# Layer B, head pairs 1 to 7: the first head's probabilities are split and turned by DMA transposes, the second head's by TensorE

## The chip, the cores and the metric

The kernel runs on one core of one Trainium2 chip. The core has TensorE (matmuls; the trace shows its matmuls as PE and its weight loads as PEld), VectorE (DVE), ScalarE (ACT), GpSimd (POOL) and SyncE (SP), which here does nothing but issue DMAs on one hardware queue, q1. The metric is the device time of one execution in microseconds (us).

## The reference, cut to what matters

The program is one step of a two-layer encoder over 2048 prompt tokens and 64 sample tokens, model width 1024. Each layer is a norm, one projection to q, k, v and a gate, an attention, and an output projection. Layer B has 16 heads of 64, and each chunk of 64 queries sees its own chunk and the 8 before it:

```
# layer B, per head and chunk of 64 queries: band = 8 * 64 + 64 keys
s = q @ k.T * dh ** -0.5 + bias[h, clip(rel, -128, 128)]
p = softmax(s)                 # over the band; keys before the start are masked
o = p @ v
y = x + (o * silu(gate)) @ w_out
```

So each query tile of 128 needs at most five key blocks of 128 (the first four tiles need 1, 2, 3 and 4), and 16 tiles have 70 blocks of 128x128 per head. To multiply by v, TensorE needs p with the keys on the partitions: p has to be transposed, block by block.

## The kernel before, in words

**Layout.** Layer A runs first, then layer B. In layer B the heads go in pairs 0 to 7 (called hp in the code). Within a pair the prompt is cut into units of two query tiles (256 queries), u = 0 to 7, and one unit of sample tokens, NU; the order is u0 to u6, NU, u7. A unit has four steps: tile 0 and tile 1 of head 0, then tile 0 and tile 1 of head 1.

**A step.** `scores` (L1375) multiplies the query tile, kept as two float16 parts, by up to 640 keys into a PSUM tile "sb" (two buffers). DVE adds the bias and takes the negated maximum into p and nm (L1412); ACT takes the exponential and the row sums (L1416). After the last step of a unit DVE takes the reciprocal of the sums (L1422), and POOL multiplies it into the gate, G (L1430). `values` transposes p on TensorE by matmuls against an identity (L840, "sb<-ident,p") into the other "sb" buffer. A product in float16 needs p as two parts: ACT copies the high part, scaled, to ph (L815), and DVE forms the low part in pl (L816). `products` multiplies both parts by v (held in "values") into one PSUM tile "o" (L1503): per head eight matmuls of 256 columns and four of 128 where all blocks are there. After the second head TensorE transposes the gate ("tp<-ident,G"), and ACT, DVE and POOL finish the output (L1243, L1245, L1246), which goes out to a buffer in memory by a DMA, ogb<-o (L1248).

**What sets the order.** TensorE's order is written by hand. A generator, the `filler`, hands out the matmuls of the projections of the next pair (L678 to L680) by a planned cost, and `pipeline` puts the steps of the attention between them: scores of step n, a piece of filler, the transposes of step n-1, with the short products (those of 128 columns and the first) of the head whose p was turned one step earlier laid between them, then that head's other products, then more filler. The other engines' instructions are ordered by a scheduler. SP issues its DMAs in that order, each with its own waits, one after another: the loads of projection inputs (xx<-xsb, 512 KB), weight loads (scan, wl), stores, and the query copies.

**Query copies.** After the second step of a unit, `queries` normalizes and turns the queries of the next unit. One half of the partitions must move to the other half, which is done by two DMAs q<-q of 32 KB (L1352). The first scores of the next unit read what the first of them writes.

Of the kernel before, what the change touches and what calls it, by code (L numbers as in the profile page):

```python
# [11 lines left out]
F16 = mybir.dt.float16  # L12
# [5 lines left out]
P = 128  # L18
# [30 lines left out]
QY = 1  # L49
NS = 4  # L50
HB, WB_, PB, VB = 2.0 ** 10, 2.0 ** 14, 2.0 ** 14, 16.0
LAG = 3
HALF = 5 * 2 * P

@with_exitstack
def hybrid_encoder_kernel(
# [162 lines left out]
    def input_across(h):  # L219
        across(h, h + 1)  # L220
        e, r, o = row[:, 16:17], row[:, 17:18], row[:, 20:23]
        powers(row[:, h : h + 1], e, r)
        times(o[:, 0:1], r, WB_)
        times(o[:, 1:2], e, 1 / (HB * WB_))
        times(o[:, 2:3], e, 0.5 / (VB * PB))

    def input_scales(h):
        everywhere(h, row[:, 20:23])
# [581 lines left out]
    def split_to(dst_hi, dst_lo, src, scale=None):  # L810
# [7 lines left out]
            )  # L818
        return a, b

    def load_cache(ktsrc, vsrc, C, both):
# [12 lines left out]
        nt = C // P  # L834
        for c in range(nt):
            split_to(VS[:, c, :, 0:HD], VS[:, c, :, HD:P], rvv[:, c])
# [415 lines left out]
    def layer_b():  # L1252
# [4 lines left out]
        def add_unit(hp, unit):  # L1257
# [21 lines left out]
            def gen():  # L1279
                xc = st.x.pop((hp, u))  # L1280
                it.prs, it.todo = [], []
                it.gate = t("pb", [P, 2, P], 5)
                if "VH" not in held:
                    held["VH"] = t("values", [P, NT, 2, P], 1, F16)
# [90 lines left out]
        def scores(it, i, h):  # L1375
# [35 lines left out]
            for r, b, c in soft:  # L1411
                mi = nc.vector.tensor_tensor_reduce(  # L1412
                    out=p[r, :nk], in0=S[r, o : o + nk], in1=b,
                    op0=ALU.add, op1=ALU.min, scale=1.0, scalar=3e38, accum_out=it.nm[r, c : c + 1],
                )
            ex = nc.scalar.activation(  # L1416
                p[:n, :nk], p[:n, :nk], AF.Exp,
                scale=-1.0, bias=it.nm[:n, c : c + 1], accum_out=it.sm[:n, c : c + 1],
            )
            bg.anchor(mi, ex)  # L1420
            if c == w - 1:
                nc.vector.reciprocal(it.sm[:n, :w], it.sm[:n, :w])  # L1422
                it.G = G = t("G", [P, 256])
                if u == NU:
                    nc.gpsimd.tensor_tensor(
# [3 lines left out]
                for e in range(len(tiles)):  # L1429
# [3 lines left out]
                        it.sm[:n, 2 * e : 2 * e + 2].unsqueeze(2).to_broadcast([n, 2, HD]),  # L1433
                        op=ALU.mult,
                    )

        def values(it, i, h, short):
            u, T, tiles = it.unit
# [21 lines left out]
            ))  # L1460

        def then(it, i, h):
            if it.unit[0] == NU:
                return [([], lambda: sample_outputs(it)), ([], lambda: sample_turned(it))]
            if i == len(it.unit[2]) - 1:
                return [products(it, h)]
            return []

        def sample_outputs(it):
            O = psum("o", 512, 1)  # L1470
# [11 lines left out]
        def sample_turned(it):  # L1482
# [5 lines left out]
            store(og[1][:, it.hp, SEQ:TOK], o)  # L1488
            finished[1, NU] = finished.get((1, NU), 0) + 1

        def products(it, h):
            u, T, tiles = it.unit
            ta, tb = tiles[0][0], tiles[1][0]
# [16 lines left out]

            def rest():
                if h == 1:
                    n = tiles[0][2]
                    GT = psum("tp", 512, 1)
                    for e, (_, t0, _) in enumerate(tiles):
                        transpose(GT[:, t0 : t0 + n], it.G[:n, e * P : (e + 1) * P])
                    gt = gate_t(GT[:, :T].rearrange("p (j s) -> p j s", j=1), T, G_B(it.hp))
                for y, x in enumerate(full):
                    if y:
                        product(x, 0)  # L1520
                    product(x, 1, stop=y == last)
                if h == 1:
                    finish_pairs(
                        it.O[:, : 2 * T].rearrange("p (j e s) -> p j e s", j=1, e=2),
                        gt,
                        T,
                        og[1][:, it.hp : it.hp + 1, u * UT : u * UT + T],
                        True,
                    )
                    finished[1, u] = finished.get((1, u), 0) + 1  # L1530

            between = [begin]
            for x in short:
# [8 lines left out]
        def pipeline():  # L1542
# [7 lines left out]
            flush()  # L1550
            filler.to(its[1].mark)
            filler.attending = True
            prev, todo = None, []
# [36 lines left out]
            values(*prev, [])  # L1590
            todo += then(*prev)
            while todo:
                filler.to(filler.done + 2.6)
                short, nxt = todo.pop(0)
                for fn in short:
                    fn()
                nxt()
            flush()

        return pipeline  # L1600
# [226 lines left out]
```

## Time and profile before

| | |
|---|---|
| runs of the kernel | 2232.93, 2240.86 and 2242.28 us, median 2240.86 |
| the profiled execution | 2242.53 us, its span 2240.8 us |
| busy in the span: TensorE, weight loads | 96%, 71% |
| busy: DVE, ACT, POOL | 70%, 63%, 38% |
| q1 | 338.10 MB, 49.1% of 16 DMA engines |

All of it is one profiled execution. The rows of the groups give line, engine, operation, output and inputs, the count, then busy us, mean ns of one and idle time before. TensorE's matmuls are pipelined: the spans of neighbours overlap, and the time that one takes away from the others is the distance between two starts. A row of the timeline starts with start and length in us. The stretch from 1200 to 1800 us lies in pairs 2 to 6 of layer B, where the same pattern repeats.

### The profile page before, as it was taken

What the parts mean: (1) busy time and instruction counts of PE and PEld (TensorE: products, weight loads), DVE (VectorE), ACT (ScalarE), POOL (GpSimd) and SP (SyncE); (2) the same over time, 40 slices, a digit from 0 to 9 for tenths busy, and PEclk for the clock granted to TensorE, in tenths of its full rate; (3) what the DMA queues carried; (4) which work ended last, traced back from release to release, by engine and by line L of the source; (5) the groups of instructions that cost most, each with busy time, mean ns of one, the idle gap of its engine ahead of it and who ended that gap; (6) DMA issues with size and microseconds to landing.
All of it is one profiled execution on the core that took longest, in us unless ns stands there. A gap on an engine that the chain in (4) does not pass through costs nothing.

```text
span 2240.8 us, 41683 instructions
## 1 busy us (share of the span) xinstructions
PE 2162.1 (96%) x13931; PEld 1580.2 (71%) x13931; DVE 1567.7 (70%) x4049; ACT 1419.6 (63%) x3610; POOL 858.4 (38%) x1397
## 2 busy tenths in 40 slices
PE   7999999999999999989999999999999999998999
PEld 6877888788889996556666666666566665566888
DVE  6768777667676456878776776867767777677542
ACT  6878778667785333666676666766666667566430
POOL 5545544334354456753333333332332323331000
PEclk9999999999999999999999999999999999999999
DMA  8856547756546666554243342533433424223664
GB/s 269 272 159 215 177 124 220 227 158 187 173 131 190 208 206 232 179 166 128 87 147 110 106 144 76 157 95 97 138 104 113 133 77 126 73 66 99 190 200 126
DMA packets 254072, 340.77 MB, mean 152 GB/s; under 512 B 45648, under 2 KB 191328, under 8 KB 253824
## 3 DMA queue, kind: packets, MB, share of 16 engines
q1 hardware_dynamic: 253856, 338.10, 49.1%
q8 instruction: 110, 1.80, 0.3%
q14 instruction: 106, 0.87, 0.1%
HBM read 257.59 MB, written 73.43 MB: 148 GB/s over the span
## 4 chain that ended last, share of the span: by engine, by line
PE 64%; DVE 13%; ACT 9%; DMA 6%; issue 5%; POOL 3%; SPq 1%; ACTq 0%; DVEq 0%; POOLq 0%
PE pj L678 11%; PE pj L680 11%; PE pj L679 11%; PE pj L1670 4%; PE pj L1672 4%; PE pj L1671 4%; PE sb L840 3%; PE o L1503 3%; PE tp L840 2%; DVE p L1412 2%; DMA scan<-in_w_in_b_dram 2%; PE sa L840 2%; ACT p L1416 2%; DVE pl L816 2%; PE sb L1408 1%
## 5 line engine op out<-in xcount | busy, mean ns | idle before, releaser
L678 PE MATMUL pj<-wh,xx 128*128 128x512 f16 (+2 forms) x1648 | 643.8, 391 | 6.2 <-ACT pb L701 4.8
L680 PE MATMUL pj<-wh,xx 128*128 128x512 f16 (+2 forms) x1648 | 626.1, 380 | 2.5 <-POOL xx L563 2.5
L679 PE MATMUL pj<-wh,xx 128*128 128x512 f16 x1024 | 390.5, 381 | 0.0
L1416 ACT ACTIVATE p<-p,nm 128x640 f32<-128x640 f32 (+5 forms) x264 | 199.5, 756 | 240.1 <-DVE nm L1412 237.5
L1670 PE MATMUL pj<-xx,wh 128*128 128x264 f32 (+1 forms) x1024 | 289.9, 283 | 5.2 <-DVE res L1676 2.2
L1671 PE MATMUL pj<-xx,wh 128*128 128x264 f32 (+1 forms) x1024 | 287.6, 281 | 0.0
L816 DVE SCALAR_TENSOR_TENSOR pl<-sb,ph 128x640 f16<-128x640 f32 (+4 forms) x256 | 189.0, 739 | 97.7 <-ACT ph L815 94.6
L679 PE MATMUL pj<-wl,xx 128*128 128x512 f32 (+1 forms) x624 | 235.7, 378 | 2.5 <-DVE wl L469 2.5
L563 POOL TENSOR_TENSOR xx<-xraw,xx 128x528 fp32r<-128x528 f32 (+4 forms) x144 | 183.9, 1296 | 87.8 <-ACT xx L562 72.8
L840 PE MATMUL sb<-ident,p 128*128 128x128 f32 x1144 | 207.6, 278 | 9.0 <-DVE pl L816 5.7
L1246 POOL TENSOR_TENSOR o<-gt,o 128x256 f32<-128x256 f32 (+1 forms) x132 | 99.9, 757 | 284.1 <-ACT p L1152 91.8
L1412 DVE CUSTOM_DVE_ANT_0 p<-sb,BT 128x640 f32<-128x640 f32 (+5 forms) x272 | 196.1, 721 | 15.5 <-PE sb L1409 10.4
L755 POOL TENSOR_TENSOR sq<-pa 128x256 f32<-128x256 f32 (+2 forms) x187 | 113.1, 605 | 226.0 <-ACT pa L714 152.5
L840 PEld LDWEIGHTS sb<-ident,p 128*128 128x128 f32 x1144 | 149.7, 142 | 68.5 <-DVE pl L816 20.7
L760 POOL TENSOR_TENSOR f<-f,mhalf 128x4 f32<-128x4 f32 (+2 forms) x187 | 192.3, 1028 | 14.1
L815 ACT ACTIVATE ph<-sb 128x640 f16<-128x640 f32 (+4 forms) x256 | 160.3, 626 | 49.8 <-PE sb L840 48.6
L680 PEld LDWEIGHTS <-xx 128*128 128x128 f16 x1024 | 100.7, 98 | 125.3 <-POOL xx L563 3.0
L1152 ACT ACTIVATE p<-p,nm 128x257 f32<-128x257 f32 (+2 forms) x272 | 134.3, 497 | 51.6 <-DVE nm L1146 44.3
L678 PEld LDWEIGHTS <-xx 128*128 128x128 f16 x1024 | 101.0, 99 | 71.4 <-issue 2.5
L679 PEld LDWEIGHTS <-xx 128*128 128x128 f16 x1024 | 100.7, 98 | 70.5 <-issue 2.3
L1503 PE MATMUL o<-pl,values 128*128 128x256 f16 (+1 forms) x672 | 149.5, 255 | 0.0
L1503 PEld LDWEIGHTS <-values 128*128 128x128 f16 x1344 | 134.8, 101 | 15.8 <-issue 0.2
(264 smaller groups left out, 5196.6 us busy)
## 6 DMA issues: line engine op xcount, KB each, us to landing
xx<-xsb SPq DMA_DIRECT2D x112, 512.0 KB, 3.8
xx<-xsa SPq DMA_DIRECT2D x88, 512.0 KB, 4.9
xraw<-oga SPq DMA_DIRECT2D x64, 264.0 KB, 3.8
xraw<-ogb SPq DMA_DIRECT2D x64, 264.0 KB, 3.8
xsa<-xx SPq DMA_DIRECT2D x32, 512.0 KB, 4.1
scan<-in_w_in_b_dram SPq DMA_DIRECT2D x64, 256.0 KB, 4.4
wl<-in_w_in_b_dram SPq DMA_DIRECT2D x64, 256.0 KB, 4.0
xraw<-in_x_dram SPq DMA_DIRECT2D x40, 256.0 KB, 3.9
```

What stands on the lines that cost most here:

```text
L563: nc.gpsimd.tensor_tensor(lo, rv, wide(hi), op=ALU.subtract)
L678: nc.tensor.matmul(ps[:n, :C], xh, wh, start=k == 0, stop=False)
L679: nc.tensor.matmul(ps[:n, :C], xh, wl, start=False, stop=False)
L680: nc.tensor.matmul(ps[:n, :C], xl, wh, start=False, stop=k == KC - 1)
L760: nc.gpsimd.tensor_tensor(fv, fv, mhalf[:n, :H], op=ALU.pow)
L816: b = nc.vector.scalar_tensor_tensor(dst_lo, src, scale, wide(dst_hi), op0=ALU.mult, op1=ALU.subtract)
L840: nc.tensor.transpose(out, in_, ident[:n, :n])
L1412: mi = nc.vector.tensor_tensor_reduce(out=p[r, :nk], in0=S[r, o : o + nk], in1=b, op0=ALU.add, op1=ALU.min, scale=1.0, scalar=3e38, accum_ ...
L1416: ex = nc.scalar.activation(p[:n, :nk], p[:n, :nk], AF.Exp, scale=-1.0, bias=it.nm[:n, c : c + 1], accum_out=it.sm[:n, c : c + 1],)
L1503: nc.tensor.matmul(it.O[:, h * T + q0 : h * T + q1_], vt, p[:, c, q0:q1_], start=start, stop=stop)
L1670: nc.tensor.matmul(ps[:, :OT], wh, oh, start=k == 0, stop=False)
L1671: nc.tensor.matmul(ps[:, :OT], wh, ol, start=False, stop=False)
```

## The change: half of the transposes go to the DMA queue

For pairs 1 to 7 and prompt units, head 0 (`TURNED = (0,)`) takes another way:

- DVE adds log PB to the negated maximum, by one more small operation per step, so that the exponential comes out scaled by PB. The row sums are then scaled too, so one more small DVE operation per unit multiplies their reciprocals by PB.
- `parts` splits p before it is turned: ACT casts the high part to float16, POOL subtracts to get the low part. Both lie in one of three slots that share the tile "values" with v.
- One step later, `turn_p` has SP issue one DMA transpose: up to ten 128x128 blocks (five of each part, 320 KB) go from the slot into the tile "pt" (two buffers). There are 112 such DMAs: seven pairs, eight units, two tiles.
- `turned_products` multiplies by v four steps after the scores of the head's second tile (`LAG = 4`).

Head 1 keeps its transposes on TensorE, but its products come one step later than before, so they are no longer laid between transposes. In these pairs the gate is transposed into an "sb" buffer instead of "tp". The list `todo` with `pop(0)` is replaced by entries with a step number, run by `due`. TensorE has 490 transposes fewer (7 x 70) and as many product matmuls as before.

```diff
-LAG = 3
+LAG = 4
 HALF = 5 * 2 * P
+TURNED = (0,)
...
+            if turned(it, h):
+                nc.vector.tensor_scalar(
+                    it.nm[:, c : c + 1], it.nm[:, c : c + 1], math.log(PB), 1.0,
+                    op0=ALU.add, op1=ALU.mult,
+                )
             ex = nc.scalar.activation(
...
+            if turned(it, h):
+                parts(it, i, h, p, nk // P)
             if c == w - 1:
                 nc.vector.reciprocal(it.sm[:n, :w], it.sm[:n, :w])
+                if turned(it, 0) and len(TURNED) == 1:
+                    part = it.sm[:n, TURNED[0] : w : 2]
+                    nc.vector.tensor_scalar(part, part, PB, 1.0, op0=ALU.mult, op1=ALU.mult)
...
+        def parts(it, i, h, p, m):
+            held["turn"] = r = (held["turn"] + 1) % 3
+            it.two = it.two if i else {}
+            it.two[i] = two = held["two"][:, 5 * r : 5 * r + m]
+            pv = p.rearrange("p (c q) -> p c q", q=P)[:, :m]
+            hi = nc.scalar.copy(two[:, :, 0, :], pv)
+            lo = nc.gpsimd.tensor_tensor(two[:, :, 1, :], pv, two[:, :, 0, :], op=ALU.subtract)
+            bg.anchor(hi, lo)
+            it.two[i] = two.rearrange("p c l q -> p (c l q)")
+
+        def turn_p(it, i, h, two):
+            if i == 0:
+                it.ph[h] = t("pt", [P, 2 * HALF], 2, F16)
+            m = two.shape[1]
+            nc.sync.dma_start_transpose(
+                it.ph[h][:, HALF * i : HALF * i + m].rearrange("p (c q) -> p c q", q=P), two
+            )
...
         def then(it, i, h):
+            late = it.hp > 0 and len(TURNED)
...
+            last = i == len(it.unit[2]) - 1
+            if turned(it, h):
+                two = it.two[i]
+                todo = [(1, "call", lambda: turn_p(it, i, h, two))]
+                return todo + [(LAG, "call", lambda: turned_products(it, h))] * last
+            return [(1, "values", (it, i, h))] + [(2 + late, "products", (it, h))] * last
...
+        def gates(it):
+            u, T, tiles = it.unit
+            n = tiles[0][2]
+            GT = psum_b("sb", 1024, 2) if it.hp and len(TURNED) else psum("tp", 512, 1)
...
-                    flush()
-                    short, nxt = todo.pop(0) if todo else ([], None)
-                    if prev is not None:
-                        values(*prev, short)
-                        bg.share(BL, BP_, KC)
-                        todo += then(*prev)
-                    prev = it, i, h
-                    if nxt is not None:
-                        nxt()
+                    due(step)
+                    todo += [(step + d, kind, o) for d, kind, o in then(it, i, h)]
+                    step += 1
```

Three places show how the instructions move. The first is SP's queue in unit 3 of pair 2, with the semaphores that each instruction waits for; xx are inputs of the projections, q the next unit's queries, ogb the finished output. Before:

```order
L526 DMA xx_16794<-xsb 128x2048 [waits DMAHW7_49,PE_49]
L526 DMA xx_16864<-xsb 128x2048 [waits DMAHW0_49,PE_49]
L1248 DMA ogb<-o_3295_16476 128x256 [waits DMAHW1_49,Pool_49]
L1352 DMA q_3300_16504<-q_3300_16504 64x256 [waits DMAHW2_49,Activation_49]
L1352 DMA q_3300_16504<-q_3300_16504 64x256 [waits DMAHW3_49,Activation_49]
L444 DMA wl_18449<-in_w_in_b_dram 128x512 [waits DMAHW4_49,DVE_49]
```

And now:

```order
L527 DMA xx_16696<-xsb 128x2048 [waits DMAHW5_49,PE_49]
L1472 DMA_TRANSPOSE pt_16387<-values_11645 128x10x128 [waits DMAHW6_49,Pool_49]
L527 DMA xx_16770<-xsb 128x2048 [waits DMAHW7_49,PE_49]
L1472 DMA_TRANSPOSE pt_16387<-values_11645 128x10x128 [waits DMAHW0_49,Pool_49]
L1360 DMA q_3262_16411<-q_3262_16411 64x256 [waits DMAHW1_49,Activation_49]
L1360 DMA q_3262_16411<-q_3262_16411 64x256 [waits DMAHW2_49,Activation_49]
L1252 DMA ogb<-o_3276_16470 128x256 [waits DMAHW3_49,Pool_49]
```

Both transposes of the unit, each waiting for POOL, stand ahead of the two query copies, and the store has moved behind these. In units 0 to 3 of a pair it is so; in units 4 and 5 the copies stand between the two transposes.

The second place is TensorE in the second step of the same unit: "sb<-ident,p" is a transpose of p, "o" a product. Before:

```order
L840 MATMUL sb_16451<-ident,p_16397 128x128
L1503 LDWEIGHTS values_11645
L1503 MATMUL o_16355<-ph_16351,values_11645 128x256
L1503 LDWEIGHTS values_11645
L1503 MATMUL o_16355<-ph_16351,values_11645 128x128
L840 MATMUL sb_16451<-ident,p_16397 128x128
L1503 LDWEIGHTS values_11645
L1503 MATMUL o_16355<-pl_16352,values_11645 128x128
```

And now, where the products read what the DMA transposes of the unit before (pt) have written:

```order
L681 MATMUL pj_16336<-wh_15132,xx_16028 128x512
L1561 LDWEIGHTS values_11645
L1561 MATMUL o_16374<-pt_16178,values_11645 128x256
L1561 LDWEIGHTS values_11645
L1561 MATMUL o_16374<-pt_16178,values_11645 128x256
L1561 LDWEIGHTS values_11645
L1561 MATMUL o_16374<-pt_16178,values_11645 128x128
L1561 LDWEIGHTS values_11645
L1561 MATMUL o_16374<-pt_16178,values_11645 128x128
```

The transposes are gone from this step, and the products in it are those of the unit before, head 0, four steps after its scores.

The third place is POOL in unit 3, for which the DMA transposes wait: f and sq belong to the norm of the projected heads, G and o to gate and output. Before:

```order
L1430 TENSOR_TENSOR G_16342<-pb_15684,sm_16178 128x128 x2
L755 TENSOR_TENSOR sq_16404<-pa_16380 128x256
L759 TENSOR_TENSOR f_16405<-f_16405,small 128x4
L760 TENSOR_TENSOR f_16405<-f_16405,mhalf 128x4
L1246 TENSOR_TENSOR o_3295_16476<-gt_16467,o_3295_16476 128x256
```

And now, with the low halves (L1464):

```order
L761 TENSOR_TENSOR f_16327<-f_16327,mhalf 128x4
L1464 TENSOR_TENSOR values_11645<-p_16358,values_11645 128x5x128
L756 TENSOR_TENSOR sq_16424<-pa_16395 128x256
L760 TENSOR_TENSOR f_16425<-f_16425,small 128x4
L761 TENSOR_TENSOR f_16425<-f_16425,mhalf 128x4
L1250 TENSOR_TENSOR o_3276_16470<-gt_16461,o_3276_16470 128x256
```

The subtractions have come in between the norm's and the output's work, one per tile of head 0.

More of the change, by code (lines that the diff above doesn't have):

```diff
@@ L224, in input_across @@
         times(o[:, 1:2], e, 1 / (HB * WB_))
-        times(o[:, 2:3], e, 0.5 / (VB * PB))
+        times(o[:, 2:3], e, 0.5 / VB if h > 0 and len(TURNED) == 2 else 0.5 / (VB * PB))
     def input_scales(h):
@@ L1489, in sample_turned, with turned_products, moving, finish @@
             finished[1, NU] = finished.get((1, NU), 0) + 1
+        def turned_products(it, h):
+            u, T, tiles = it.unit
+            ta, tb = tiles[0][0], tiles[1][0]
+            ka, kb = max(ta - 4, 0), max(tb - 4, 0)
+            if h == 0:
+                it.O = psum("o", 512, 1)
+            def moving(kt, low):
+                if kt > ta:
+                    return it.ph[h][:, HALF + 2 * P * (kt - kb) + P * low :][:, :P], P, UT
+                c = it.ph[h][:, 2 * P * (kt - ka) + P * low :][:, :P]
+                if kt < kb:
+                    return c, 0, P
+                return (
+                    bass.AP(
+                        tensor=c.tensor, offset=c.offset,
+                        ap=[c.ap[0], [HALF - 2 * P * (kb - ka), 2], c.ap[-1]],
+                    ),
+                    0, UT,
+                )
+            for kt in [kb] + [k for k in range(ka, tb + 1) if k != kb]:
+                for low in range(2):
+                    x, q0, q1_ = moving(kt, low)
+                    nc.tensor.matmul(
+                        it.O[:, h * T + q0 : h * T + q1_], held["VH"][:, kt, h], x,
+                        start=kt == kb and not low, stop=kt == tb and low == 1,
+                    )
+            if h == 1:
+                gates(it)
+                finish(it)
+        def gates(it):
+            u, T, tiles = it.unit
+            n = tiles[0][2]
+            GT = psum_b("sb", 1024, 2) if it.hp and len(TURNED) else psum("tp", 512, 1)
+            for e, (_, t0, _) in enumerate(tiles):
+                transpose(GT[:, t0 : t0 + n], it.G[:n, e * P : (e + 1) * P])
+            it.gt = gate_t(GT[:, :T].rearrange("p (j s) -> p j s", j=1), T, G_B(it.hp))
+        def finish(it):
+            u, T, tiles = it.unit
+            finish_pairs(
+                it.O[:, : 2 * T].rearrange("p (j e s) -> p j e s", j=1, e=2),
+                it.gt,
+                T,
+                og[1][:, it.hp : it.hp + 1, u * UT : u * UT + T],
+                True,
+            )
+            finished[1, u] = finished.get((1, u), 0) + 1
         def products(it, h):
@@ L1512, in rest @@
                 if h == 1:
[L1513 to L1517, printed above, removed]
+                    gates(it)
                 for y, x in enumerate(full):
@@ L1552, in pipeline, with due @@
             filler.attending = True
-            prev, todo = None, []
+            todo, step = [], 0
+            def due(at):
+                flush()
+                now = [x for x in todo if x[0] <= at]
+                todo[:] = [x for x in todo if x[0] > at]
+                short, rests, vals = [], [], []
+                for _, kind, x in now:
+                    if kind == "products":
+                        between, rest = products(*x)
+                        short += between
+                        rests.append(rest)
+                    else:
+                        {"values": vals, "call": rests}[kind].append(x)
+                for x in vals:
+                    values(*x, short)
+                    bg.share(BL, BP_, KC)
+                for fn in short + rests:
+                    fn()
             for x, it in enumerate(its):
@@ L1589, in pipeline @@
                 assert x + 2 >= len(its) or its[x + 2].ready
-            values(*prev, [])
-            todo += then(*prev)
             while todo:
                 filler.to(filler.done + 2.6)
[L1594 to L1597, printed above, removed]
+                due(step)
+                step += 1
             flush()
```

27 lines of the change are left out of this document (14 added, 13 removed).

## The prediction

> **What bounds the kernel now.** I read the page's head first, then the table of windows over the middle of layer B, then TensorE's list of waits there.
>
> ```profile
> span 2240.8 us, 41683 instructions
> PE 2162.1 (96%) x13931; PEld 1580.2 (71%) x13931; DVE 1567.7 (70%) x4049; ACT 1419.6 (63%) x3610; POOL 858.4 (38%) x1397
> ...
> L840 PE MATMUL sb<-ident,p 128*128 128x128 f32 x1144 | 207.6, 278 | 9.0 <-DVE pl L816 5.7
> ```
>
> ```profile
> core 0: us, PE busy (x) PEld busy (x) DVE busy (x) ACT busy (x) POOL busy (x), PEclk, DMA share, GB/s
> 1200.00:1350.00 150.00, 147.11 (x932) 90.84 (x930) 112.48 (x281) 97.72 (x252) 48.53 (x87) 1.00 0.36 111
> ...
> sum 600.00, PE 589.28 PEld 363.99 DVE 446.34 ACT 392.49 POOL 198.21; mean PE 147.32 PEld 91.00 DVE 111.58 ACT 98.12 POOL 49.55
> ```
>
> ```profile
> PE sb L840 <- DVE pl L816: 4.1, 13, 0.9
> PE tp L840 <- DVE scl L212: 3.9, 4, 1.1
> PE tp L840 <- ACT gt L1233: 2.4, 4, 0.8
> PE sb L840 <- DVE nm L1412: 1.5, 4, 0.4
> PE tp L211 <- DVE KB L1363: 0.2, 1, 0.2
> ...
> DVE most L174 <- DMA scan<-in_w_in_b_dram: 23.6, 16, 3.5
> ...
> DVE most L174 <- DMA scan<-in_w_o_b_dram: 8.5, 8, 1.8
> ```
>
> TensorE is busy 147.3 of every 150 us, at a granted clock of 1.00, and its waits between 1050 and 1800 us sum to 12.1 us (last fence, total, times, longest), so layer B is TensorE's own work. DVE idles a quarter of the time, ACT a third, POOL two thirds. Work taken off TensorE therefore shortens the span by TensorE's own time, until something that it waits for comes late.
>
> **The change part by part.** *The transposes that go.* Head 0 of seven head pairs has 70 blocks of 128x128 per pair (of sixteen query tiles, twelve have 5 and the first four 1, 2, 3 and 4), 490 in all. The group above says 278 ns each, but those spans overlap; what one costs is the distance between starts:
>
> ```profile
> 1244.70 0.71 PE L840 MATMUL sb<-ident,p 128*128 128x128 f32 x5
> 1245.24 0.38 PE L678 MATMUL pj<-wh,xx 128*128 128x512 f16 x1
> ...
> 1218.79 0.22 PE L1408 MATMUL sb<-KA,q 128*128 128x128 f16 x1
> 1234.17 0.33 PE L1408 MATMUL sb<-KA,q 128*128 128x384 f16 x1
> 1251.75 0.33 PE L1408 MATMUL sb<-KA,q 128*128 128x384 f16 x1
> 1271.00 0.33 PE L1408 MATMUL sb<-KA,q 128*128 128x384 f16 x1
> ```
>
> Five take 1245.24 - 1244.70 = 0.54 us, 0.108 each. 490 x 0.108 = 52.9 us (by 278 ns it would be 136, which counts the overlaps twice). The products stay: as many matmuls of as many columns as before. With half of the transposes gone, half of the 4.1 us that they wait for DVE goes too, 2.05 in 750 us; the seven pairs last some 980 us (7 x 8 units of 17.4, a third of the way from 1218.79 to 1271.00, where the last four rows start units 1 to 4 of pair 2), so 2.7 us.
>
> *DVE, ACT, POOL.* Rows of the groups kept apart by shape:
>
> ```profile
> L816 DVE SCALAR_TENSOR_TENSOR pl<-sb,ph 128x640 f16<-128x640 f32 x192 | 157.7, 822 | 70.9 <-ACT ph L815 68.1
> L815 ACT ACTIVATE ph<-sb 128x640 f16<-128x640 f32 x192 | 133.0, 693 | 37.9 <-PE sb L840 37.0
> L563 POOL TENSOR_TENSOR xx<-xraw,xx 128x512 f16<-128x512 f32 x32 | 39.5, 1253 | 2.2 <-ACT xx L562 2.2
> L1422 DVE RECIPROCAL sm<-sm 128x4 f32<-128x4 f32 x64 | 11.3, 176 | 23.9 <-ACT p L1416 22.7
> ```
>
> DVE loses 84 splits of 0.82 and 28 smaller ones and gains 168 small operations (112 shifts of the maximum, 56 scalings of the sums) that I price by the reciprocal, 0.18: 30 us against 69 and more, a gain that nothing waits for. One shift stands in the chain to the exponential and delays it 0.18; the next scores are two steps off, so it costs nothing. ACT swaps 112 splits for 112 casts of the same size, 0.69: zero; if a cast from SBUF differs, ACT's idle third covers it. POOL takes the low half, never seen here: the nearest row is its subtraction of 512 columns, 1.25, so 640 columns are 1.57 and all of it 490 x 0.313 = 153 us, POOL going from 33% to about 49%. It is paid on the way to the DMA, not by TensorE.
>
> *The DMA transposes.* SP gets 112 new instructions, two per unit, on its one queue, in order. What stands behind them matters: by the order of SP, in units 0 to 3 of each pair the copies of the next unit's queries stand behind both transposes, in 4 and 5 behind one. The scores that open the next unit need those copies. From the timelines of pair 2, the first tile's scores or exponentials, the second's, and the copies (first row unit 1, then three of unit 2, four of unit 3), and below them the query tile's landing times, the DMA table from 1200 to 1800 us and SP's first wait there:
>
> ```profile
> 1221.92 0.27 PE L1408 MATMUL sb<-KA,q 128*128 128x256 f16 x1
> 1236.33 0.83 ACT L1416 ACTIVATE p<-p,nm 128x640 f32<-128x640 f32 x1 [0.83 <-DVE nm L1412]
> 1240.02 0.83 ACT L1416 ACTIVATE p<-p,nm 128x640 f32<-128x640 f32 x1 [1.84 <-DVE nm L1412]
> 1243.71 1.31 SPq L1352 DMA_DIRECT2D q<-q  x2
> 1254.31 0.83 ACT L1416 ACTIVATE p<-p,nm 128x640 f32<-128x640 f32 x1 [1.46 <-DVE nm L1412]
> 1255.43 0.33 PE L1408 MATMUL sb<-KA,q 128*128 128x384 f16 x1
> 1258.25 0.83 ACT L1416 ACTIVATE p<-p,nm 128x640 f32<-128x640 f32 x1 [1.97 <-DVE nm L1412]
> 1263.21 0.47 SPq L1352 DMA_DIRECT2D q<-q  x1
> ...
> DMA to landing us min/median/max: 1.7/2.0/3.5
> ...
> q1 hardware_dynamic: 41492, 67.51, 36.9%
> ...
> xx<-xsb SPq DMA_DIRECT2D x66, 512.0 KB, 3.8
> ...
> ogb<-o SPq DMA_DIRECT2D x33, 128.0 KB, 1.9
> ...
> q<-q SPq DMA_DIRECT2D x66, 32.0 KB, 2.0
> ...
> SPq L526 <- PE pj L680: 207.5, 41, 9.8
> ```
>
> The exponentials of unit 2 end at about 1237.2 and 1240.9. Cast and subtraction add 0.69 + 1.57 and some tenths for the semaphores and POOL's other work, so the two transposes can be issued at about 1240.0 and 1243.7. The next unit starts at 1251.75; two sets of five transposes less put that at 1250.67, and with 2.0 us of landing the first copy must leave by 1248.7. In unit 3 the same sum, from the exponentials at 1254.31 and 1258.25, gives 1257.6 and 1261.7 for the transposes and 1271.00 - 1.08 - 2.0 = 1267.9 for the copy. In unit 1, with 3 and 4 blocks, they come some 5 us after their scores (unit 2: 1240.0 - 1234.17 = 5.8, its operations being longer), at 1223.8 and 1227.2, and the copy has to leave by 1234.17 - 7 x 0.108 - 2.0 = 1231.4.
>
> Let s be the time for which one full transpose (two halves of five blocks, 320 KB) keeps back what SP issues next, and 0.3 the load between. At s = 4 the second transpose of unit 2 is through at 1240.0 + 8.3 = 1248.3, 0.4 us in time. Its price isn't in the trace. Low end: it passes like one copy, 0.33 us of issue and some 2.9 to land (between 128 KB at 1.9 and 512 KB at 3.8). Far end: ten blocks of 128x128, each landing as the 32 KB copy does, 2.0, one after another, 20 us. Between them I take ten block issues of 0.33 to 0.47, as SP's rows of a whole copy and a query copy have it, s = 4, nearest to the row of the 512 KB transfer, 3.8. A quicker one would gain no more than the next two terms.
>
> *Queries late.* At s = 4 there are 0.4 us to spare in unit 2, and the readiness of POOL can be off by that: I take 0.4 per pair, 3 us.
>
> *Other loads late.* SP waits a lot for TensorE (207.5 us in 600 for one kind of load), so there is room: per unit some nine issues of 0.33 to 0.47, 3.6 us, and 8 us of transposes in 16.3. But a load that becomes due finds the queue held half of the time, with 2 us left, so it comes 1 us later on average, an estimate. The weight scans are what DVE already waits for: 24 times, 32.1 us. They would wait 24 us more; TensorE has waited 12.1 where DVE waited 32.1 for these, so 24 x 0.38 = 9 in 750 us, and 10 over the seven pairs, where the longer stretch stands against DVE's lighter work (ends: 0, and all of it over 980 us, 31).
>
> *Turned products.* They come four steps after the last scores of their head, at unit 3's second step, not before 1255.43 - 1.08 = 1254.4; the transpose lands at about 1243.7 + 0.3 + 4 + 2 = 1250. Cover 4 us. Their PSUM tile and the store behind them move a step or two; the store's reader is the output projection of another stage: zero. The gate's transposes move to the pool of the scores, which loses two of eight tiles per unit and gains one: zero. The last unit's products fall one step later, under the output projections: zero, at most a step of 4.
>
> Sum, against the profiled run's 2242.5 (span 2240.8, and 1.7 around it; the median of the runs, 2240.9, is the same within their spread): -52.9 - 2.7 + 3 + 10 = -42.6, **2200 us**.
>
> One rule speaks against this. The rows above show 0.108 us of TensorE per block and 320 KB that would pass in 3 us as a copy. The Trainium skill's page "VectorE: DVE Perf Modes", section "The three transpose paths", has one 128x128 transpose at 390 ns on TensorE and 1309 ns through the DMA crossbar, and advises TensorE wherever PSUM can take the result. On TensorE's figure the trace differs (0.108 between starts, 0.278 for one). Worked out from its crossbar figure, an estimate, a full transpose here is 10 x 1.309 = 13.1 us. The page "DMA: Bandwidth & Descriptors" (section "Latency and other measured facts") instead has 261 GB/s for such a transfer on one kernel, an estimate of 1.3 us here, with which the sum would be some 2190.
>
> **The rivals.** *Slower: the transposes hold the queue for 8 us.* SP issues each block's descriptors itself, or the queue finishes a transpose before it starts the next transfer. Then unit 1 starts its successor 1223.8 + 0.6 x 8 + 0.8 x 8 - 1231.4 = 3.6 us late, unit 2 1256.3 - 1248.7 = 7.6, unit 3 1257.6 + 16 - 1267.9 = 5.7: 16.9 per pair, 118 in all, and 2242.5 - 55.6 + 118 + 10 = **2315**. It decides from s = 6 on, where the three sum to about 6 to 7 per pair, which is the gain. For it: ten blocks per instruction; against it: q1's packets take 36.9% of the DMA engines' time here, which leaves them room.
>
> *Most of it given back:* s between 5 and 6 leaves 1.6 to 6 us per pair, 11 to 42 in all, and 2208 to 2242: around **2230**.
>
> *Slower by far: block after block.* If a block costs 1.0 us, half of what the 2.0 of the smallest copy allows, a pair's 140 blocks (both halves) hold SP's queue for 140 us, and its other 8 x 3.6 = 29 make 169 where a pair takes 8 x 17.4 = 139 now: 30 x 7 = 210 more, **2450**; at 2.0 each it is 3430. It decides from about 0.8 us per block. Against it: a copy of 512 KB takes 3.8 us and one of 32 KB 2.0, so size costs little in the copies of this trace. The first page's rule is this case: by its figure, 183 + 29 - 139 = 73 per pair, about 2750.
>
> *All kept:* s under 3, no load late: 2242.5 - 55.6 + 3 = **2190**, within the forecast's own range, 2184 to 2225.
>
> **How the numbers follow.** Half a per cent, 11 us, is about what a measurement of this kernel can tell from no change. Forecast with all kept 0.50; most given back 0.13 (0.05 of it still over 0.5% faster, 0.07 within, 0.01 slower); queue held for 8 us 0.26; block after block 0.11. So faster 0.55, within 0.5% 0.07, slower 0.38. The price s is unknown over a factor of sixty and the kernel breaks even at 6, so the chance of a loss is large though the likeliest is a gain. The range goes from 2184 (all kept and DVE's relief counted once more) to 2325, s a little over 8, which leaves out the block case and the upper end of the third, about 0.18.
>
> **What would show it.** Right: the table of DMA issues has the transpose landing in under 5 us, and SP's next issue follows in under 5; the row of TensorE's transposes into the score pool falls by 490; its waits for the query copies stay under 1 us per unit; a pair lasts 5 to 7 us less. Wrong: the chain or the waits show the scores' line waiting for the copy q<-q, above all in units 1 to 3; SP's row of the transposes is several us long; or the products of the turned head wait for the transpose, which needs s over 8 or POOL late. POOL over 60%, or its subtraction over 2 us, would move all the ready times by as much and cost from 0.4 us on.

## The result, and the profile after

| | runs | median, us | ratio to the kernel before |
|---|---|---|---|
| before | 4 | 2238.56 (2232.93 to 2242.28) | |
| changed | 4 | 2215.45 (2214.71 to 2218.44) | 0.9901, 95% interval 0.9876 to 0.9926 |

The change gains 1.0%, 22 us by the ratio, about half of the forecast 42.6. The time lies in the range and in the likeliest case's own range (2184 to 2225). The profile of the changed kernel, first the page's head and the groups of POOL's low halves and of TensorE's transposes into the score pool, then the same window as before:

```profile
span 2213.1 us, 41369 instructions
PE 2102.7 (95%) x13441; PEld 1522.1 (69%) x13441; DVE 1563.9 (71%) x4105; ACT 1425.7 (64%) x3610; POOL 1004.9 (45%) x1509
...
L1464 POOL TENSOR_TENSOR values<-p,values 128x640 f16<-128x640 f32 x84 | 117.8, 1403 | 211.9 <-ACT values L1463 211.9
L844 PE MATMUL sb<-ident,p 128*128 128x128 f32 x654 | 103.2, 277 | 28.1 <-DVE nm L1420 14.0 <-DVE pl L817 10.2 <-ACT values L719 2.3
```

```profile
core 0: us, PE busy (x) PEld busy (x) DVE busy (x) ACT busy (x) POOL busy (x), PEclk, DMA share, GB/s
...
1200.00:1350.00 150.00, 142.89 (x879) 85.51 (x878) 110.31 (x291) 100.91 (x257) 71.40 (x108) 0.99 0.57 150
```

TensorE is now busy 142.9 of 150 us where it was busy 147.1: the transposes are gone (654 of 1144 are left, 490 fewer), and some of their time has become idle time. Its waits from 1050 to 1800 us were 12.1 us in total; now they are 36.3:

```profile
PE sb L844 <- DVE nm L1420: 11.4, 5, 2.3
PE sb L1416 <- DVE nm L1420: 8.9, 7, 1.7
PE tp L844 <- DVE pa L774: 8.0, 5, 1.7
PE sb L844 <- DVE pl L817: 5.1, 6, 1.1
PE sb L844 <- ACT gt L1237: 1.5, 3, 0.9
PE tp L844 <- DVE scl L213: 1.0, 4, 0.3
PE pj L679 <- ACT pb L723: 0.4, 1, 0.4
```

None of them is a wait for a DMA. Every one is for a result of DVE or ACT, most come once per head pair at the same place (five pairs lie in that stretch), and the third did not exist in this stretch before: the transposes of the next queries wait for the norm (L774). The DMA transposes, in the DMA table from 1200 to 1800 us and then, from SP's timeline, in two neighbouring issues:

```profile
q1 hardware_dynamic: 120225, 88.26, 56.8%
...
q<-q SPq DMA_DIRECT2D x68, 32.0 KB, 2.2
...
pt<-values SPq DMA_TRANSPOSE x69, 3.6
```

```profile
1250.99 1.46 SPq L1472 DMA_TRANSPOSE pt<-values  x1
1252.54 1.32 SPq L1360 DMA_DIRECT2D q<-q  x2
```

A transpose holds SP for about 1.4 us and lands after 3.6, and the query copies behind it are issued at once and land nearly as fast as before (2.2 against 2.0). So no loss is to be seen in the queue that the prediction worked on.

By pairs (from the timelines, the distance between the first scores of the sample unit in one pair and in the next) seven pairs take 1022.3 us before and 1000.9 after. TensorE's waits in this stretch, the same list over 1032.1 to 2054.4 and 1024.9 to 2025.8 us, sum to 23.3 us before and 54.6 after. What is left is TensorE's own time: 999.0 before and 946.3 after. It fell by 52.7 us, and the waits took 31.3 of that back.

These 21.4 us are most of the 27.7 between the two profiled spans. Another 7.2 lie ahead of pair 0's sample unit, where nothing is turned by DMA. There the two executions differ in the granted clock, 0.98 before and 0.99 after from 0 to 1020 us, which by itself is worth about as much (1020 x 0.01 = 10 us, an estimate).

### The profile page after: what moved, and what is told of

It is laid out like the page before. It is cut to its first block, busy times and chain, and to the rows that moved or that the text cites. A ratio compares the mean times of both kernels' runs of the same rounds, so it can differ in the third digit from the quotient of the medians.

```text
span 2213.1 us, 41369 instructions
## 1 busy us (share of the span) xinstructions
PE 2102.7 (95%) x13441; PEld 1522.1 (69%) x13441; DVE 1563.9 (71%) x4105; ACT 1425.7 (64%) x3610; POOL 1004.9 (45%) x1509
## 5 line engine op out<-in xcount | busy, mean ns | idle before, releaser
L1464 POOL TENSOR_TENSOR values<-p,values 128x640 f16<-128x640 f32 (+2 forms) x112 | 140.0, 1250 | 243.5 <-ACT values L1463 243.5
L761 POOL TENSOR_TENSOR f<-f,mhalf 128x4 f32<-128x4 f32 (+2 forms) x187 | 187.0, 1000 | 13.8
L774 DVE TENSOR_TENSOR pa<-pa,f 128x256 f32<-128x256 f32 (+3 forms) x221 | 136.5, 618 | 55.1 <-POOL f L761 50.6
L756 POOL TENSOR_TENSOR sq<-pa 128x256 f32<-128x256 f32 (+2 forms) x187 | 123.7, 663 | 72.5 <-ACT pa L715 38.2
L817 DVE SCALAR_TENSOR_TENSOR pl<-sb,ph 128x640 f16<-128x640 f32 (+4 forms) x144 | 106.2, 737 | 58.2 <-ACT ph L816 56.5
L1767 PE MATMUL pj<-xx,wl 128*128 128x264 f32 x512 | 145.0, 283 | 1.0 <-DVE wl L463 1.0
L1767 PE MATMUL pj<-xx,wh 128*128 128x264 f16 x512 | 142.1, 277 | 1.3 <-DVE wh L460 1.3
L1150 DVE CUSTOM_DVE_ANT_0 p<-sa,BT,nsink 128x256 f32<-128x256 f32 (+2 forms) x272 | 117.3, 467 | 34.6 <-PE sa L844 29.5
```

What stands on the lines that cost most here:

```text
L761: nc.gpsimd.tensor_tensor(fv, fv, mhalf[:n, :H], op=ALU.pow)
L774: nc.vector.tensor_tensor(sv, sv, fv.unsqueeze(2).to_broadcast([n, H, HD]), op=ALU.mult)
L1464: lo = nc.gpsimd.tensor_tensor(two[:, :, 1, :], pv, two[:, :, 0, :], op=ALU.subtract)
L1767: nc.tensor.matmul(ps[:, :OT], wl, oh, start=False, stop=k == KC - 1)
```

## The experiments

Twelve kernels ran, in three groups on three chips: e1 to e4, e5 to e8, e9 to e12. The kernel before took 2229.9, 2235.4 and 2235.3 us there, so ratios are compared; 0.1% is 2.2 us. A step of a few tenths of a per cent between two groups is therefore less sure than its intervals say. The last columns help there: the length of the seven pairs in each kernel's profiled execution, and TensorE's waits in it. The kernel before has 1022.3 and 23.3, the changed one 1000.9 and 54.6; e9 is the changed kernel again, so two executions of one kernel can lie 4.2 us apart.

| run | edit to the changed kernel | ratio to before | 95% interval | seven pairs, us | waits, us |
|---|---|---|---|---|---|
| e1 | POOL's low half no anchor | 0.9839 | 0.9812 to 0.9866 | 981.9 | 36.9 |
| e2 | second portions handed out | 1.0032 | 1.0016 to 1.0047 | 1020.6 | 60.0 |
| e3 | no DMA transposes, new order kept | 1.0048 | 1.0033 to 1.0063 | 1025.3 | 31.7 |
| e4 | plain copies in place of transposes | 0.9919 | 0.9893 to 0.9945 | 1004.7 | 56.2 |
| e5 | no DMA transposes, only the gate moved | 1.0012 | 0.9996 to 1.0027 | 1023.0 | 26.9 |
| e6 | both heads turned, e1's edit | 1.0124 | 1.0093 to 1.0156 | 1045.6 | 124.3 |
| e7 | e1, three steps, head 1's old place | 0.9926 | 0.9903 to 0.9948 | 1005.3 | 55.3 |
| e8 | each DMA transpose issued twice | 1.0075 | 1.0052 to 1.0097 | 1031.6 | 79.3 |
| e9 | none | 0.9897 | 0.9882 to 0.9912 | 996.7 | 54.4 |
| e10 | e1 and e2 | 0.9895 | 0.9879 to 0.9912 | 992.3 | 43.0 |
| e11 | e6 and e2 | 0.9961 | 0.9946 to 0.9976 | 1007.5 | 91.5 |
| e12 | e1, three steps | 0.9916 | 0.9900 to 0.9932 | 1001.2 | 49.2 |

**Theories.** Theory 1: the missing 25 us of the profiled runs went into the order of DVE's and POOL's work. Theory 2: into the queue, by the DMA transposes. Theory 3: into the new order of TensorE's own steps.

**e4, the transposing itself.**

```diff
-            nc.sync.dma_start_transpose(
-                it.ph[h][:, HALF * i : HALF * i + m].rearrange("p (c q) -> p c q", q=P), two
-            )
+            nc.sync.dma_start(it.ph[h][:, HALF * i : HALF * i + m], two)
```

> Each DMA transpose is a plain DMA copy of the same 320 KB instead, so head 0 of pairs 1 to 7 multiplies probabilities that are not turned; everything else stands. Theory 2 (turning on the DMA engines costs: 58% of their time where it was 49%, 3.6 us to land and 1.2 to 2.4 on SP): the time falls by 8 to 25 us, to 2190 to 2207. Theory 1: the same within 4 us, 2211 to 2219.

A plain copy of the same bytes holds SP for 0.48 us and lands in 2.6 (the tile's own query):

```profile
L1472 SPq DMA_DIRECT2D pt<-values x68: 478/484/617, 1210.9 to 1799.8; - x68
...
DMA to landing us min/median/max: 1.8/2.6/5.4
```

So turning costs 0.9 us of SP and 1.0 us of landing per transfer, and the whole kernel is no faster without it: 0.9919 against 0.9901 and 0.9897 (e9). Theory 2 falls for the turning. The copies still put the same bytes and issues on the queue; that these do no harm is read from the waits of the changed kernel, where TensorE waits for no DMA. Ten blocks at 1309 ns each, 13.1 us by an estimate from the Trainium skill's page "VectorE: DVE Perf Modes", section "The three transpose paths", aren't what the trace shows: a transpose lands in 3.6 us, 1.0 more than a copy.

**e1, what stands behind POOL's low half.** The background work (weights, norms) is given to the scheduler behind an anchor, the last marked instruction of its engine. The change marks a POOL instruction for the first time: the low half, which waits for ACT's cast.

```diff
-            bg.anchor(hi, lo)
+            bg.anchor(hi)
```

> The background work is tied behind the last anchored instruction of its engine; here POOL's low half is no longer an anchor, so the norm's operations on POOL needn't stand behind it. Theory 1 (the missing 25 us went into DVE and POOL doing things in a worse order, the DMA transposes themselves cost nothing): POOL's wait at the low half for the cast (176 us between 1050 and 1800 us) falls below 100, TensorE's wait tp<-DVE pa (1.6 us per pair) goes, and the time falls by 5 to 12 us, to about 2206. Theory 2 (the queue: transposes delay loads and copies): unchanged within 4 us, 2215.

In the changed kernel, at the end of one pair, POOL sat 7.24 us in front of the low half; the norm's steps behind it (sq, f) came after, so DVE's L774 was late and TensorE waited 1.58 us for the queries:

```profile
1463.76 1.40 POOL L1464 TENSOR_TENSOR values<-p,values 128x640 f16<-128x640 f32 x1 [7.24 <-ACT values L1463]
1465.12 1.19 POOL L756 TENSOR_TENSOR sq<-pa 128x256 f32<-128x256 f32 x2
...
1469.86 0.76 DVE L774 TENSOR_TENSOR pa<-pa,f 128x256 f32<-128x256 f32 x1
...
1470.67 0.44 PE L844 MATMUL tp<-ident,pa 128*128 128x128 f32 x2 [1.58 <-DVE pa L774]
```

In e1, at the same place, the norm is done first and the low half waits 0.25:

```profile
1457.06 1.01 POOL L761 TENSOR_TENSOR f<-f,mhalf 128x4 f32<-128x4 f32 x1
1458.32 1.47 POOL L1464 TENSOR_TENSOR values<-p,values 128x640 f16<-128x640 f32 x1 [0.25 <-ACT values L1463]
```

TensorE's longest waits in e1, and POOL's first, from 1050 to 1800 us:

```profile
PE sb L844 <- DVE nm L1420: 11.1, 5, 2.2
PE sb L844 <- DVE pl L817: 4.4, 5, 1.1
PE sb L844 <- ACT gt L1237: 4.3, 5, 1.1
PE sb L1416 <- DVE nm L1420: 3.3, 6, 1.1
...
POOL values L1464 <- ACT values L1463: 109.5, 69, 4.4
```

POOL's wait there falls from 175.8 (the same view of the changed kernel) to 109.5 us, not below the 100 that was expected. The wait tp<-DVE pa is gone, the scores' wait for the maximum (L1416) falls from 8.9 to 3.3 us, TensorE's waits fall from 36.3 to 25.3 us in all, and the time falls by 0.6%: e1 stands at 0.9839 against 0.9901 and 0.9897. That is 13 us, more than the 5 to 12 expected; in the seven pairs e1 is 15 (e9) to 19 us shorter. e1 is the fastest kernel of the study, 2191.6 us on a chip where the kernel before took 2229.9.

The first wait of e1's list stays as it was, 2.2 us once per pair. Around one of these waits DVE is busy without a break, 2.00 of 2.00 us in each of four windows from 1427.29 to 1435.29, so what TensorE waits for stands behind other work of DVE there.

DVE's order holds one thing more that the prediction had priced at 0.18 us: the shift of the maximum (L1425). Near 1290 us in e1 the maximum is read out at 1289.98 and the shift starts at 1292.62, 2.6 us later, behind four other operations. Most shifts follow within 0.5 us (65 of 112 in e1). No run shows what the late ones cost.

**e9, the changed kernel again.**

> The changed kernel once more, so that the kernels of this chip stand beside it: a ratio of 0.988 to 0.993 to the kernel before, as in its first comparison.

0.9897, as in the first comparison, so the changed kernel's ratio held in another group. It did not run on e1's chip; there e4, which keeps its order, stood at 0.9919.

**e3 and e5, the new order without DMA transposes.** In e3 `TURNED = ()`, head 1's (and here head 0's) products stay a step late and the gate stays in the score pool; in e5 only the latter.

```diff
-TURNED = (0,)
+TURNED = ()
...
-            late = it.hp > 0 and len(TURNED)
+            late = it.hp > 0          # e3 alone
...
-            GT = psum_b("sb", 1024, 2) if it.hp and len(TURNED) else psum("tp", 512, 1)
+            GT = psum_b("sb", 1024, 2) if it.hp else psum("tp", 512, 1)
```

> No head is turned by DMA (all transposes on TensorE again), but the products come one step later and the gate is transposed into the score pool, as in the changed kernel. Theory 3 (the new order alone costs: seven tiles per unit alternate in two PSUM buffers and the gate takes one from the scores): 2238 plus 15 to 30, about 2260. Theories 1 and 2: the order costs under 6 us, 2238 to 2244.

> All transposes on TensorE and the products when they came before; of the new order only the gate's transposes in the score pool are left. Order alone (e3) cost 0.48%, 10.7 us. If the gate in the score pool is that cost (seven tiles alternating in two buffers), 0.3 to 0.6% slower than before; if the later products are (no longer laid between transposes), within 0.15%.

e3 is 0.48% slower than before, 10.7 us: under Theory 3's 15 to 30, over the 6 of the other two. e5 is 0.12% slower with an interval that holds zero, so by the ratios the gate's move can't be told from free, and the later products, of both heads here, are most of e3's cost, 8 us. The profiles say less. The seven pairs are 3.0 us longer in e3 than before, and 0.7 in e5. TensorE's waits there grow by 8.4 and by 3.6 us, while its granted clock is 1.00 in both where it was 0.99 before. So the later products do add waits, and their price stays open between 2 us (e3's pairs less e5's) and 8.

From e3 to e1 half of the transposes go to the DMA: 1.0048 to 0.9839, 2.09% or 47 us, and 43.4 in the seven pairs. That is the price of 490 transposes on TensorE less what the DMA's way costs where nothing is tied behind POOL. The order does not stay wholly the same: head 0's products come four steps after their scores in e1, and a unit hands out two portions of background work fewer.

**e12 and e7, a shorter way to the products.**

```diff
-LAG = 4
+LAG = 3
...
-            late = it.hp > 0 and len(TURNED)
+            late = 0                  # e7 alone
```

> e1 with the turned products three steps after the scores and head 1's products left late. If the earlier turned products made e7 19 us slower than e1 (they wait for the transpose): the same here, 0.990 to 0.995. If putting head 1's products back between the transposes did: like e1, 0.981 to 0.986.

> As e1, but the turned products come three steps after their scores and head 1's products at their old place, laid between the transposes. The transposes land 3.6 us after issue, so three steps (12 us) should hold them. If the later products cost most of e3's 10.7 us: 6 to 11 us faster than e1, ratio 0.979 to 0.981. If the gate does: within 3 us of e1, ratio 0.983 to 0.985.

Both have e1's edit and are 17 (e12) and 19 us (e7) slower than e1, which neither case of e7's expectation had; their intervals overlap. In the seven pairs they are 19 and 23 us longer, with 12 and 18 us more waits. So head 1's old place brings nothing here, and the three steps cost. It is not that the transposes land too late: TensorE's wait for pt in e12 is 0.4 us in 750. It waits oftener for DVE (10.1 us on the low half of head 1, 19 times, where e1 has 4.4 in five). Why its order came out worse stays open. That e3's cost could be had back is therefore not shown.

**e2 and e10, the portions of background work.** After each `values` a portion is handed out; a step whose transposes are gone has only the one after the scores.

```diff
                 for fn in short + rests:
                     fn()
+                if not vals:
+                    bg.share(BL, BP_, KC)
```

> In the steps in which head 0 no longer has transposes, the changed kernel hands out one portion of background work where before there were two (6 per unit, not 8). Here a step without transposes hands out its second portion again. Theory 1 (the portions left out pile up in units 4 to 7 of a pair, where DVE then takes 15.4 of 17.5 us and TensorE waits for the maximum): those waits (1.7 + 2.3 + 1.1 us per pair) fall under 2 us, the time falls by 10 to 22 us, to about 2198. Theory 2 (the queue): unchanged within 4 us.

> e1 and e2 together: POOL's low half is no anchor, and steps without transposes hand out their second portion of background work. Theory A (e2 was slower because the earlier portions bring the weights' scale into a worse place, TensorE's wait tp<-DVE scl of 2.7 us once per pair and a lower granted clock after it): slower than e1 by 8 to 25 us, ratio 0.988 to 0.996, with that wait. Theory B (e2 was slower because more norm work was tied behind POOL's low half): with the tie gone it is like e1 or better, 0.978 to 0.985.

Theory 1's form in e2 fell: it is 29 us slower than the changed kernel (1.0032 to 0.9901). The wait at 2.3 us per pair stayed, and a new one came, for the scale of the next weights, 2.8 us once per pair. TensorE's granted clock is low after it, as the windows of 2 us around one such wait show (columns as above: the clock is the third from the end). Over the whole profiled execution it is 0.983 where the changed kernel has 0.991, worth up to 18 of the 29 us (2237 x 0.008, an estimate). First the waits, then the windows:

```profile
PE sb L844 <- DVE nm L1420: 11.2, 5, 2.4
PE tp L844 <- DVE scl L213: 11.0, 4, 2.8
```

```profile
1254.69:1256.69 2.00, 0.00 (x0) 0.00 (x1) 1.70 (x3) 0.26 (x2) 2.00 (x3) 0.87 1.04 254
1256.69:1258.69 2.00, 2.00 (x9) 1.48 (x10) 0.56 (x2) 1.20 (x4) 0.34 (x1) 0.50 0.81 195
1258.69:1260.69 2.00, 2.00 (x12) 0.96 (x11) 1.77 (x5) 1.74 (x5) 0.46 (x2) 0.78 0.35 74
```

With the tie gone (e10) that wait goes too (1.0 us in 750), yet e10 is 0.56% slower than e1, as Theory A said, though not by its wait. Of the 24 us between the two profiled spans, 11 lie ahead of pair 0's sample unit and 10 in the seven pairs. Ahead, the edit acts once: the first step of pair 0 has no transposes either, so it hands out a portion there too, and near the start of the pair TensorE waits for the norm where e1 waits 0.53 us:

```profile
908.10 0.69 PE L844 MATMUL tp<-ident,pa 128*128 128x128 f32 x2 [4.77 <-DVE pa L774]
```

From 850 to 1020 us the granted clock is then 0.93, in e1 0.97. With one head turned, more portions make it worse; they are not what was missing.

**e8, how much room the queue has.**

```diff
+            for _ in range(2):
                 nc.sync.dma_start_transpose(
```

> The changed kernel with each DMA transpose issued twice into the same place, the second behind the first's landing, so that a transpose keeps SP for some 5 us (s of the prediction = 5). By the prediction's sum queries would be late by 0 to 2 us per pair and other loads later: 2 to 25 us over the changed kernel (ratio 0.991 to 1.002). If the queue has wide room: within 3 us, ratio 0.989 to 0.992. If it is near its edge: over 30 us more, ratio above 1.004.

1.0075, 39 us over the changed kernel, beyond the sum's 2 to 25 and in the case "near its edge". Waits in e8 from 1050 to 1800 us, of TensorE (the first three lines), SP and DVE:

```profile
PE sb L1416 <- issue: 13.8, 5, 3.8
...
PE o L1562 <- DMA pt<-values: 4.4, 4, 2.2
PE sb L1416 <- DMA q<-q: 2.2, 3, 1.4
...
SPq L1473 <- DMA pt<-values: 90.3, 77, 3.1
...
DVE most L175 <- DMA scan<-in_w_in_b_dram: 50.3, 29, 3.8
```

Here is what the prediction feared: scores that wait (2 to 4 us, once per pair, and behind the copies by name), products that wait for the transpose, and scans that DVE waits for 50.3 us where the changed kernel has 17.9. The first line has no releaser in the profile, but the longest of its waits ends with a copy: issued at 1770.26, it takes 4.9 us to land, and the scores start at 1775.29. In the seven pairs e8 is 31 us longer than the changed kernel, 25 of it in TensorE's waits.

A doubled transpose keeps SP some 4.9 us, as meant: 3.5 to land and 1.35 for the second issue (medians). But the order on SP moved too. In units 1 to 3 of pair 2 the copies now stand behind the first tile's two transposes and ahead of the second tile's, where in the changed kernel they stand behind both tiles'.

**e6 and e11, both heads.** `TURNED = (0, 1)`, in both e1's edit, in e11 also e2's.

> Both heads are turned by DMA, POOL's low half not an anchor (as in e1). Going on from e1: TensorE loses 490 more transposes, 53 us, DVE 69, and POOL gains 153 us, to some 64%. Theory A (TensorE is still the bound, and the queue has room): 2150 to 2170 on the scale of 2230 for the kernel before, ratio 0.965 to 0.975. Theory B (POOL's chain to the DMA, and norms behind it, bind, and the queue holds four transposes per unit): no faster than e1, ratio 0.984 to 1.02.

> e6 with the second portions handed out again. In e6 TensorE waited for weights that ACT and DVE prepare (23.7 + 19.9 us from 1050 to 1800 us), as only four portions per unit are left. Theory A (those portions are what made e6 slow): the waits for weights fall under 5 us and the time by 40 to 80 us, ratio 0.975 to 0.995. Theory B (four transposes per unit are too much for queue, POOL and DMA engines, at 73% of their time): ratio over 1.003.

Theory A of e6 fell: 1.0124, slower than before. TensorE's first waits in e6, and then one of e11:

```profile
PE pj L679 <- ACT wh L467: 23.7, 11, 4.0
PE pj L680 <- DVE wh L470: 19.9, 15, 2.6
```

```profile
PE sb L1416 <- DMA q<-q: 15.8, 6, 2.8
```

In e6 the weights come late, for there are four portions per unit left where there were eight. e11 hands them out, and these waits go, with 36 us, a little less than the 40 to 80 expected. What remains in e11 (the last line) are, among others, queries that come late; they share the queue with four transposes per unit.

TensorE's own time in the seven pairs is indeed shorter, 921.3 us in e6 against 945.0 in e1, although its granted clock is only 0.95 there and 0.99 in e1. The waits of 124.3 us eat it up. So neither version with both heads beats one head.

## Why the prediction was right or wrong

**The bound and the transposes: right.** TensorE was the bound, and the 490 transposes were priced well: 52.9 us in the sum, against 52.7 us less own time of TensorE in the seven pairs, and 56.7 in e9.

**TensorE's waits: the step that failed.** The sum let them fall by 2.7 and put 13 on top for queries and loads, all of it by way of the queue. They grew by 31.3 us, and none of it is a wait for a DMA. That the forecast was still only double the gain is in part luck, since the 13 that did not come stood in for a part of what was not priced.

**"ACT, DVE, POOL" and POOL's work "paid on the way to the DMA, not by TensorE": wrong.** This is the largest part of it. The subtraction's length was nearly right (1.40 us against 1.57), but it stands in order on POOL ahead of the norm of the next queries, and it waits for the cast. The prediction named the chain to the transpose and not what is queued behind the waiting instruction. Price: 13 us by the ratios, and 17.7 of the 31.3 us of waits (54.6 in the changed kernel, 36.9 in e1).

**s, the price of a transpose: right in kind, too high in size.** The sum took 4 us from ten block issues. Measured: 1.4 us on SP, 3.6 to land, copies behind it undisturbed. That is near the low end, so "Queries late" (3) was 0. "Other loads late" (10) has no trace either: DVE's wait for the weight scans fell from 32.1 to 21.5 us (17.9 and 3.6). The way in which it would go wrong was right: with s at 5 (e8) copies and scans are late. The loss there, 39 us, is larger than the 2 to 25 by the sum; why the sum falls short is not shown.

**The order of TensorE's steps: half unpriced.** The turned products and the gate were put at zero, and the gate can't be told from it (e5). That head 1's products come one step later was not priced at all. With both heads' products late and no DMA transposes (e3 less e5) it costs 8 us by the ratios and 2 in the profiles; for head 1 alone no run shows it.

**What stays open.** In e1, where nothing is tied behind POOL, TensorE still waits 13.6 us more in the seven pairs than before, above all 2.2 us per pair for DVE's maximum. It is not the missing portions of background work (e2, e10). A lower clock follows some of these waits. And small changes of order move this kernel by 10 to 20 us whose cause nobody found (e10, e12), so a step of 13 us is no proof by itself. For the tie it is the waits that went with it that speak.

**The signs.** The transposes landed and SP went on in under 5 us, 490 transposes are gone, and no wait for the copies is in the list: as the prediction asked. A pair became 3.1 us shorter, not 5 to 7.

**The rivals.** The queue held for 8 us, and block after block, did not happen. "Most of it given back" came half true, for another reason. (The upper end of that case, 2242, should by its own terms be 2239.)

## What to carry to other kernels

An instruction moved to an idle engine can cost what stands behind it in that engine's order, from the moment when it begins to wait, and not only its own length: ask of each engine what is queued behind the newcomer, and who needs that. Where a helper ties other work to "the last marked instruction", a new mark moves that work as well. When the bound engine's work gets shorter, its waits for the next engines can grow, here by 31 us of the 53 saved, so part of the gain is to be booked as lost before it is measured. And compare own time and waits apart: the saving was right to within 4 us here, and the error lay in the waits.

## What the runs showed of the hardware that was not expected

- A DMA transpose, mostly of 320 KB in one instruction, holds SP for 1.36 us and lands in 3.6 us (medians), against 0.48 and 2.6 to 2.7 for copies of the same size.
- After a wait of 2.7 us TensorE's granted clock was 0.50 and 0.78 in the next two windows of 2 us (e2, above); in e1, after 2.22 us, 0.69, 0.50 and 0.95. In the changed kernel one wait of 2.31 us was followed by 0.78, 0.50 and 0.87, and another of the same length by 1.00 throughout. Between 1160 and 1800 us none of its twelve waits of 1.0 to 1.7 us was followed by less than 1.00; in pair 0, where waits of 1.35, 1.49 and 0.51 us lie within 6 us, 0.93, 0.50 and 0.72 came after. So a wait of over 2 us costs up to 1.7 us more, sometimes (0.22, 0.50 and 0.13 of 2 us each in the changed kernel). The Trainium skill's page "TensorE: Matmul & The Clock Gate", Part 1, has the clock halved after an idle window of some 3.4 us; here shorter waits do it.
